# Reordering the seven down products of a fp32 decoder trunk, with the next layer's value weights spread over two of them

## The chip, the cores and the metric

One NeuronCore of a Trainium2 chip runs the whole program. The metric is the device time of one execution in microseconds, lower is better; the median of the runs is compared.

## The reference

The program computes two decoder layers for 512 tokens of width 1024 in float32. Each layer normalizes its input, projects it, runs differential attention and forgetting attention, projects back, normalizes and adds; then comes the FFN, and only its last line and the norm around it matter here:

```python
h = rms_norm(x, ffn_pre_g[l])
y = (jax.nn.silu(h @ w_gate[l]) * (h @ w_up[l])) @ w_down[l]
x = x + rms_norm(y, ffn_post_g[l])
```

With `D_FF` = 2816, the down projection is a 512 x 2816 by 2816 x 1024 product. The next layer begins with `h = rms_norm(x, attn_pre_g[l + 1])` and the projection of the value heads, `va`.

## The kernel before

Every float32 operand is split in a high part (`fp32r`) and a low part, the rest. ScalarE (ACT) makes the high part with a cast, VectorE (DVE) the low part with a subtraction (`load_w`, lines 258 and 259, for weights; `split`, lines 263 and 264, for the rest), and TensorE (PE) runs three matmuls for each product: high by high, high by low, low by high.

The down product is done as seven products of half size (Strassen's scheme in Winograd's form): the 2816 rows of the weight and the hidden activations are cut in two halves of 11 blocks, the tokens in two halves of 256 and the output columns in two of 512. Sums of activations are made while gate and up run (`swiglu`, from line 1236); some stay in SBUF as operands `op0q` to `op3q`, the others go to DRAM (`s_d`) and come back with `reload` (line 1326) into the operand buffers that have been read. Sums of weight blocks lie in DRAM (`t_d`), made by `weight_sums`.

A product (line 1320) runs over six chunks of weights (`chunk_w`, line 1297): five of two blocks (128 x 1024) and one of one block. A chunk's 12 matmuls (6 for the last) are 6 for the first 128 tokens of the half, m = 0, then 6 for m = 1; 66 in a product. The code's call `product(banks, g, x)` names the two PSUM banks, the operand group g and the weight side x. In the trace the matmuls are `da`, `db` or `dc` by the banks `A_`, `B_` or `C_`. In the order of a program below, a chunk is named by layer, side and number: `wl_d073` is the low part of chunk 3 of side 7 in layer 0. Even chunks are loaded into two buffers `wr`, odd ones into two buffers `xr`; high and low parts have three buffers each, so that the cast of a chunk waits for the PE to finish the chunk three before it. For the first four products `xr` shares the two buffers of the gains (tag `gain`); for the later ones `xr` takes the operand buffers `op32` and `op33`, which the fourth product reads.

The seven products stand in the code in this order (group, side): (0, 4) in `A_`, (1, 6) in `C_`, (2, 1) in `A_`, (3, 0) in `B_`, (0, 2) in `A_`, (1, 7) in `B_`, (2, 3) in `A_`. Below they are the first to the seventh product. Between them DVE adds banks into half tiles `u`, `u3`, `p5`, `y2`, which end as the four blocks of the result: the first 256 tokens (t = 0 and 1) have their second column half when the sixth product is done, and the last 256 tokens (t = 2 and 3) get theirs with the sixth and seventh.

`post_norm` (line 304) then sums the squares on ACT (`square_sum`, line 277), lets GpSimd (POOL) make the root in two steps (lines 271 and 272, `v` and `r`), and adds the scaled result to the residual `xs` on DVE (line 316); in the last layer each half is stored from there. `pre_norm` (line 279) does the same for the next layer's input (`h_a`, line 286), and `pre_T` transposes it on PE.

The last three chunks of the seventh product (`TAIL = 3`) run first for m = 0 and then for m = 1. After them come the 96 matmuls of the next layer's `va`, four token tiles t by four pieces c of the weight. Those weights are loaded (`wvr`) and split (`wvh`, `wvl`) into operand buffers that are free by then, named by `VA_TAGS`: for each of the four pieces c the buffer of the raw data, of the high and of the low part. In the next layer `vd_split` reads the banks of `va` into `vd_h` (ACT, line 386) and `vd_l` (DVE, line 387), which gives the four banks free for the projections (`pj_kd` is the first).

All instructions of an engine run in the order in which they were built; the tile framework's scheduler chooses that order from the code's order and its own costs. All loads are issued by SyncE (SP), in its own order too.

Of the kernel before, what the change touches and what calls it, by code (L numbers as in the profile page):

```python
# [11 lines left out]
F32 = mybir.dt.float32  # L12
# [23 lines left out]
TB = S // 16  # L36
VA_C, VA_T = 4, 1
TAIL = 3
VA_TAGS = (("34", "02", "03"), ("34", "04", "10"), ("30", "11", "12"), ("34", "13", "14"))
KSPLIT = 4  # L40
EPS = 1e-6
BIG = 1e30
# [132 lines left out]
def hymba_block(ctx, tc, x_d, pos_d, apre_d, win_d, fb_d, lq1_d, lk1_d, lq2_d, lk2_d, dsg_d, wout_d, apost_d,  # L175
# [171 lines left out]
    for l in range(DEPTH):  # L347
# [849 lines left out]
        with ExitStack() as fctx:  # L1197
# [155 lines left out]
                V.tensor_add(u[m], A_[m], u[m])  # L1353
            reload(1, 1)
            product(B_, 3, 0)
            p5, y = (hp.tile([P, 2, S], F32, name=f"{x}{l}", tag=f"op3{q}") for q, x in enumerate(("p5", "y0")))
            g_fpost = gain(fpost_d, l, f"g_fpost{l}")
            if l + 1 < DEPTH:
                g_apre = gain(apre_d, l + 1, f"g_apre{l + 1}")
            for m in range(2):  # L1360
                A.copy(p5[:, m], B_[m])
            reload(2, 2)
            for t in range(2):
                ys[t] = y[:, t]
                V.tensor_mul(ys[t], c11[t], g_fpost[:, CH[0]])
            product(A_, 0, 2)
            u3, y2 = (hp.tile([P, 2, S], F32, name=f"{x}{l}", tag=f"op0{q}") for q, x in enumerate(("u3", "y2")))
            for m in range(2):
                V.tensor_add(u3[:, m], A_[m], u[m])
                V.tensor_add(u[m], p5[:, m], u[m])  # L1370
            product(B_, 1, 7)
            last = l + 1 == DEPTH
            for m in range(2):
                V.tensor_add(u[m], B_[m], u[m])
            for t in range(2):
                post_norm(t, u[t], s2s[t], g_fpost, name, y=ys[t], store=last)
                if not last:
                    hs[t] = pre_norm(t, g_apre, f"a{l + 1}")
            for m in range(2):
                ys[2 + m] = y2[:, m]  # L1380
                V.tensor_add(ys[2 + m], u3[:, m], p5[:, m])
                s2s[2 + m] = first_half(2 + m, ys[2 + m], name, z=1)
                V.tensor_mul(ys[2 + m], ys[2 + m], g_fpost[:, CH[1]])
            product(A_, 2, 3, range(QN - TAIL))
            ws = [chunk_w(3, q) for q in range(QN - TAIL, QN)]
            if not last:
                for c in range(4):
                    raw, hi, lo = (hp.tile([P, 2, S], dt, name=f"wv{x}{l}{c}", tag=f"op{tag}") for x, dt, tag in zip(
                        "rhl", (F32, F32R, F32R), VA_TAGS[c]))
                    src = win_d[l + 1][2 * c * P:(2 * c + 2) * P, VA:VA + S].rearrange("(k p) n -> p k n", p=P)  # L1390
                    nc.sync.dma_start(raw, src)
                    split(hi, lo, raw)
                    for k in range(2):
                        wva[2 * c + k] = hi[:, k], lo[:, k]
            pinned[0] = True
            a = f"a{l + 1}"
            for m in range(2):
                t = 2 + m
                for w, q in zip(ws, range(QN - TAIL, QN)):
                    product_mm(A_[m], 2, q, w, m)  # L1400
                    if m and not last and q == QN - TAIL:
                        pre_T(0, hs[0], a)
                c21 = half_tile(f"c21{l}{m}")
                V.tensor_add(c21, A_[m], u3[:, m])
                post_norm(t, c21, s2s[t], g_fpost, name, z=0, y=ys[t], store=last)
                if not last:
                    hs[t] = pre_norm(t, g_apre, a)
            if not last:
                va(0, 0, 1)
                pre_T(1, hs[1], a)  # L1410
# [29 lines left out]
```

## Time and profile before

| what | us |
|---|---|
| three runs | 1244.06, 1246.26, 1253.99 |
| median | 1246.26 |
| the profiled execution | 1249.71 |
| its span, first to last instruction | 1247.9 |

The profiled execution is 3.45 us above the median, and 1.8 us of it lie around the span. PE is busy 96% of the span. Busy time of PE is modelled from the matmuls' issue, so a stretch in which PE counts as busy can still be longer than its matmuls need; the start of the first matmul of one product to the start of the first of the next is the measure used below.

### The profile page before, as it was taken

What the parts mean: (1) busy time and instruction counts of PE and PEld (TensorE: products, weight loads), DVE (VectorE), ACT (ScalarE), POOL (GpSimd) and SP (SyncE); (2) the same over time, 40 slices, a digit from 0 to 9 for tenths busy, and PEclk for the clock granted to TensorE, in tenths of its full rate; (3) what the DMA queues carried; (4) which work ended last, traced back from release to release, by engine and by line L of the source; (5) the groups of instructions that cost most, each with busy time, mean ns of one, the idle gap of its engine ahead of it and who ended that gap; (6) DMA issues with size and microseconds to landing.
All of it is one profiled execution on the core that took longest, in us unless ns stands there. A gap on an engine that the chain in (4) does not pass through costs nothing.

```text
span 1247.9 us, 16724 instructions
## 1 busy us (share of the span) xinstructions
PE 1201.7 (96%) x5817; PEld 989.3 (79%) x5817; DVE 817.3 (65%) x1574; ACT 599.2 (48%) x1162; POOL 210.4 (17%) x250
## 2 busy tenths in 40 slices
PE   8999999999999999999799999999999999999996
PEld 5787877788888888887687878777988888887875
DVE  7697858665554545576848977695755455555855
ACT  5476757553333233365544767674533233324643
POOL 1302457320000000000223124572200000000001
PEclk9999999999999999999999999999999999999999
DMA  7333443416575766798504333434167676677863
GB/s 231 91 85 93 112 115 105 136 37 196 188 238 182 227 203 211 251 313 264 171 2 119 90 89 93 121 110 125 62 192 242 196 214 212 208 233 247 294 203 125
DMA packets 211268, 206.75 MB, mean 166 GB/s; under 512 B 11680, under 2 KB 155680, under 8 KB 211184
## 3 DMA queue, kind: packets, MB, share of 16 engines
q1 hardware_dynamic: 211040, 205.16, 53.2%
q8 instruction: 46, 0.75, 0.3%
q10 hardware_dynamic: 144, 0.52, 0.1%
q14 instruction: 38, 0.31, 0.1%
HBM read 163.34 MB, written 33.91 MB: 158 GB/s over the span
## 4 chain that ended last, share of the span: by engine, by line
PE 44%; issue 32%; DVE 13%; ACT 4%; DMA 4%; POOL 2%; SPq 0%; POOLq 0%; DVEq 0%; ACTq 0%
PE pj_g L205 10%; PE pj_u L205 10%; PE o L205 4%; PE va L205 3%; PE pj_kf L205 2%; PE pj_kd L205 2%; PE da L205 2%; PE pj_qf L205 2%; DMA rs<-s_d 2%; PE vb L205 1%; DVE t2kd L739 1%; PE db L205 1%; PE ptf L210 1%; DVE ed L958 1%; PE of L205 1%
## 5 line engine op out<-in xcount | busy, mean ns | idle before, releaser
L205 PE MATMUL pj_g<-hT_h,wh_g 128*128 128x512 f32 (+1 forms) x384 | 142.9, 372 | 0.0
L205 PE MATMUL pj_g<-hT_l,wh_g 128*128 128x512 f32 (+1 forms) x384 | 142.6, 371 | 0.0
L205 PE MATMUL pj_g<-hT_h,wl_g 128*128 128x512 f32 (+1 forms) x384 | 142.6, 371 | 0.0
L205 PE MATMUL pj_u<-hT_h,wh_u 128*128 128x512 f32 (+1 forms) x368 | 140.1, 381 | 0.0
L205 PE MATMUL pj_u<-hT_l,wh_u 128*128 128x512 f32 (+1 forms) x368 | 139.8, 380 | 0.0
L205 PE MATMUL pj_u<-hT_h,wl_u 128*128 128x512 f32 (+1 forms) x368 | 139.8, 380 | 0.0
L271 POOL TENSOR_SCALAR v_fp<-s_fp 128x1 f32<-128x1 f32 x8 | 5.2, 651 | 685.4 <-ACT junk L277 354.7
L259 DVE TENSOR_TENSOR wl_u<-wr_u,wh_u 128x1024 fp32r<-128x1024 f32 x44 | 53.9, 1225 | 98.5 <-ACT wh_u L258 98.5
L258 ACT CAST wh_g<-wr_g 128x1024 fp32r<-128x1024 f32 x44 | 46.4, 1054 | 145.9 <-PE pj_u L205 86.9
L205 PE MATMUL da<-wh_d,op 128*128 128x512 f32 x352 | 111.3, 392 | 2.1 <-ACT wh_d L258 2.1
L258 ACT CAST wh_u<-wr_u 128x1024 fp32r<-128x1024 f32 x44 | 46.3, 1053 | 135.4 <-PE pj_g L205 128.3
L1239 DVE TENSOR_TENSOR sg<-pj_u,sg 128x512 f32<-128x512 f32 x44 | 30.4, 690 | 80.8 <-PE pj_u L205 80.8
L205 PEld LDWEIGHTS pj_g<-hT_h,wh_g 128*128 128x128 f32 x384 | 72.4, 188 | 12.7
L205 PEld LDWEIGHTS pj_g<-hT_h,wl_g 128*128 128x128 f32 x384 | 72.2, 188 | 12.5
L205 PEld LDWEIGHTS pj_g<-hT_l,wh_g 128*128 128x128 f32 x384 | 72.3, 188 | 12.3
L205 PE MATMUL da<-wl_d,op 128*128 128x512 f32 x176 | 69.7, 396 | 10.9 <-DVE wl_d L259 10.9
L205 PEld LDWEIGHTS pj_u<-hT_h,wl_u 128*128 128x128 f32 x368 | 69.2, 188 | 13.2
L205 PEld LDWEIGHTS pj_u<-hT_h,wh_u 128*128 128x128 f32 x368 | 69.2, 188 | 13.1
L205 PEld LDWEIGHTS pj_u<-hT_l,wh_u 128*128 128x128 f32 x368 | 69.2, 188 | 12.9
L205 PEld LDWEIGHTS da<-wh_d,op 128*128 128x128 f32 x352 | 66.4, 189 | 16.4 <-ACT wh_d L258 2.9
L258 ACT CAST wh_d<-wr_d 128x1024 fp32r<-128x1024 f32 x42 | 44.2, 1052 | 42.4 <-PE da L205 15.4
L259 DVE TENSOR_TENSOR wl_d<-wr_d,wh_d 128x1024 fp32r<-128x1024 f32 x42 | 51.3, 1222 | 19.2 <-ACT wh_d L258 18.6
(301 smaller groups left out, 3019.1 us busy)
## 6 DMA issues: line engine op xcount, KB each, us to landing
wr_g<-in_w_gate_dram SPq DMA_DIRECT2D x44, 512.0 KB, 4.4
wr_u<-in_w_up_dram SPq DMA_DIRECT2D x44, 512.0 KB, 4.6
b<-in_w_down_dram SPq DMA_DIRECT2D x88, 256.0 KB, 3.6
t_d<-b SPq DMA_DIRECT2D x88, 256.0 KB, 4.0
wr_d<-t_d SPq DMA_DIRECT2D x24, 512.0 KB, 4.9
wr_d<-in_w_down_dram SPq DMA_DIRECT2D x18, 512.0 KB, 5.0
wr_o<-in_w_out_dram SPq DMA_DIRECT2D x16, 512.0 KB, 4.4
xr<-t_d SPq DMA_DIRECT2D x16, 512.0 KB, 5.1
```

The costliest lines, as they stand in the source:

```text
L205: ins = PE.matmul(out, a, b, start=start, stop=stop)
L210: ins = PE.transpose(out, a, idn)
L258: A.copy(hi, raw)
L259: (eng or V).tensor_sub(lo, raw, hi.bitcast(F32))
L271: G.tensor_scalar(v, s2[:, 0:1], scalar1=s2[:, 1:2], scalar2=EPS, op0=ALU.add, op1=ALU.add)
L739: return V.tensor_mul(b["t2"], b["t2"], sinT)
L958: return V.scalar_tensor_tensor(e0, e0, b["r"][:, 0:1], e1, op0=ALU.mult, op1=ALU.add)
L1239: V.tensor_mul(sg, pu, sg)
```

## The change

The last three products become (1, 7) in `C_`, (0, 2) in `B_`, (2, 3) in `A_`. The first 256 tokens are whole after the fifth product. The copy `p5` and the tiles `u3` and `y2` go; `w5` holds the sum of the fourth product and `u`, and `c12` the finished column half of the first tokens. The norm of t = 0 and the value pieces 0 and 1 stand in the code before the sixth product's sums are read, the norm of t = 1 and the pieces 2 and 3 behind the seventh product's chunks. The pieces take other operand buffers.

```diff
-VA_TAGS = (("34", "02", "03"), ("34", "04", "10"), ("30", "11", "12"), ("34", "13", "14"))
+VA_TAGS = (("34", "10", "11"), ("14", "12", "13"), ("34", "00", "01"), ("04", "02", "03"))
...
             product(B_, 3, 0)
-            p5, y = (hp.tile([P, 2, S], F32, name=f"{x}{l}", tag=f"op3{q}") for q, x in enumerate(("p5", "y0")))
+            w5, y = (hp.tile([P, 2, S], F32, name=f"{x}{l}", tag=f"op3{q}") for q, x in enumerate(("w5", "y0")))
+            for m in range(2):
+                V.tensor_add(w5[:, m], B_[m], u[m])
+            reload(2, 2)
+            product(C_, 1, 7)
             g_fpost = gain(fpost_d, l, f"g_fpost{l}")
...
-                A.copy(p5[:, m], B_[m])
-            reload(2, 2)
-            for t in range(2):
-                ys[t] = y[:, t]
-                V.tensor_mul(ys[t], c11[t], g_fpost[:, CH[0]])
-            product(A_, 0, 2)
-            u3, y2 = (hp.tile([P, 2, S], F32, name=f"{x}{l}", tag=f"op0{q}") for q, x in enumerate(("u3", "y2")))
-            for m in range(2):
-                V.tensor_add(u3[:, m], A_[m], u[m])
-                V.tensor_add(u[m], p5[:, m], u[m])
-            product(B_, 1, 7)
...
+                ys[m] = y[:, m]
+                V.tensor_mul(ys[m], c11[m], g_fpost[:, CH[0]])
+                V.tensor_add(c12[m], C_[m], w5[:, m])
+            product(B_, 0, 2)
+            a = f"a{l + 1}"
+
+            def end(t, x, z):
+                post_norm(t, x, s2s[t], g_fpost, name, z=z, y=ys[t], store=last)
                 if not last:
-                    hs[t] = pre_norm(t, g_apre, f"a{l + 1}")
...
+            end(0, c12[0], 1)
+            values_w(0, 1)
+            for m in range(2):
+                ys[2 + m] = w5[:, m]
+                V.tensor_add(ys[2 + m], B_[m], w5[:, m])
+                V.tensor_add(u[m], B_[m], u[m])
+            product(A_, 2, 3, range(QN - TAIL))
+            ws = [chunk_w(3, q) for q in range(QN - TAIL, QN)]
+            end(1, c12[1], 1)
+            values_w(2, 3)
+            for m in range(2):
+                s2s[2 + m] = first_half(2 + m, ys[2 + m], name, z=1)
+                V.tensor_mul(ys[2 + m], ys[2 + m], g_fpost[:, CH[1]])
...
-                V.tensor_add(c21, A_[m], u3[:, m])
+                V.tensor_add(c21, A_[m], u[m])
```

`values_w(*cs)` holds the loop over the pieces that stood there before, word for word. Where the instructions now stand is shown at three places, before first and after second.

SP in layer 0, from the first chunk of the fifth product on: `wr`, `xr` are weight chunks, `rs` the reloaded operands, `g_` the gains, `wvr` the value weights.

```order
L257 DMA wr_d020_5485<-t_d0_3047 128x2x512
L1331 DMA rs024_5473<-s_d0_3048 128x2x256
L236 DMA g_fpost0_5447<-in_ffn_post_g_dram 128x1024
L1331 DMA rs025_5478<-s_d0_3048 128x256
L257 DMA wr_d022_5521<-t_d0_3047 128x2x512
L236 DMA g_apre1_5449<-in_attn_pre_g_dram 128x1024
L257 DMA xr021_5503<-t_d0_3047 128x2x512
L257 DMA xr023_5539<-t_d0_3047 128x2x512
```

```order
L257 DMA wr_d070_5479<-in_w_down_dram 128x2x512
L1331 DMA rs024_5469<-s_d0_3048 128x2x256
L1331 DMA rs025_5474<-s_d0_3048 128x256
L257 DMA wr_d072_5515<-in_w_down_dram 128x2x512
L257 DMA xr071_5497<-in_w_down_dram 128x2x512
L257 DMA xr073_5533<-in_w_down_dram 128x2x512
L257 DMA wr_d074_5551<-in_w_down_dram 128x2x512
L1383 DMA wvr00_5716<-in_w_in_dram 128x2x512
```

The two gains went from ahead of the second chunk to behind the sixth; the first value piece follows the fifth chunk.

DVE in layer 0 during the sixth product (`wl_d07` before, `wl_d02` after): `wvl` are value pieces, `y1_fp`, `xs` and `h_a` the steps of a token tile's norms.

```order
L259 TENSOR_TENSOR wl_d073_5649<-xr073_5647,wh_d073_5648 128x1024
L1381 TENSOR_TENSOR y20_5588<-u30_5587,p50_5445 128x512 x2
L264 TENSOR_TENSOR wvl01_5833<-wvr01_5831,wvh01_5832 128x1024
L259 TENSOR_TENSOR wl_d074_5667<-wr_d074_5665,wh_d074_5666 128x1024
L259 TENSOR_TENSOR wl_d075_5685<-xr075_5683,wh_d075_5684 128x512
```

```order
L259 TENSOR_TENSOR wl_d023_5647<-xr023_5645,wh_d023_5646 128x1024
L316 SCALAR_TENSOR_TENSOR xs_78<-y1_fp00_5695,r_fp00_5697,xs_78 128x512
L264 TENSOR_TENSOR wvl01_5724<-wvr01_5722,wvh01_5723 128x1024
L264 TENSOR_TENSOR wvl02_5829<-wvr02_5827,wvh02_5828 128x1024
L259 TENSOR_TENSOR wl_d024_5665<-wr_d024_5663,wh_d024_5664 128x1024
L259 TENSOR_TENSOR wl_d025_5683<-xr025_5681,wh_d025_5682 128x512
L286 SCALAR_TENSOR_TENSOR h_a100_5703<-xs_78,r_a10_5710,g_apre1_5583 128x512
L286 SCALAR_TENSOR_TENSOR h_a101_5704<-xs_78,r_a10_5710,g_apre1_5583 128x512
L313 TENSOR_TENSOR y1_fp01_5806<-c1201_5586,g_fpost0_5581 128x512
```

The norm of the first token tile and half of that of the second have come into this product, and so has one more value piece.

DVE in layer 0 from the first chunk of the seventh product (`wl_d030`) on.

```order
L259 TENSOR_TENSOR wl_d030_5755<-wr_d030_5753,wh_d030_5754 128x1024
L264 TENSOR_TENSOR wvl03_5845<-wvr03_5843,wvh03_5844 128x1024
L1374 TENSOR_TENSOR u00_5063<-db00_4959,u00_5063 128x512
L1374 TENSOR_TENSOR u01_5064<-db01_4960,u01_5064 128x512
L313 TENSOR_TENSOR y1_fp00_5699<-u00_5063,g_fpost0_5447 128x512
L259 TENSOR_TENSOR wl_d031_5773<-xr031_5771,wh_d031_5772 128x1024
L316 SCALAR_TENSOR_TENSOR xs_78<-y00_5446,r_fp00_5701,xs_78 128x512
L316 SCALAR_TENSOR_TENSOR xs_78<-y1_fp00_5699,r_fp00_5701,xs_78 128x512
L259 TENSOR_TENSOR wl_d032_5791<-wr_d032_5789,wh_d032_5790 128x1024
```

```order
L259 TENSOR_TENSOR wl_d030_5734<-wr_d030_5732,wh_d030_5733 128x1024
L316 SCALAR_TENSOR_TENSOR xs_78<-y1_fp01_5806,r_fp01_5808,xs_78 128x512
L1392 TENSOR_TENSOR w50_5445<-db00_4959,w50_5445 128x512
L1393 TENSOR_TENSOR u00_5063<-db00_4959,u00_5063 128x512
L1392 TENSOR_TENSOR w50_5445<-db01_4960,w50_5445 128x512
L1393 TENSOR_TENSOR u01_5064<-db01_4960,u01_5064 128x512
L259 TENSOR_TENSOR wl_d031_5752<-xr031_5750,wh_d031_5751 128x1024
L259 TENSOR_TENSOR wl_d032_5770<-wr_d032_5768,wh_d032_5769 128x1024
L286 SCALAR_TENSOR_TENSOR h_a110_5814<-xs_78,r_a11_5821,g_apre1_5583 128x512
```

Ahead of the second chunk's low part there now stand four adds that read the sixth product's banks; the steps of the norms behind it are fewer.

## Rows read from the trace of the kernel before

**Rows 1.** Stretches: us; busy PE, PEld, DVE, ACT, POOL (instructions); PEclk, DMA share, GB/s.
```profile
572.53:590.25 17.72, 15.56 (x67) 12.31 (x66) 8.34 (x8) 8.27 (x10) 0.00 (x0) 1.00 0.81 263
590.25:605.22 14.97, 14.97 (x68) 12.39 (x66) 11.17 (x14) 7.32 (x8) 0.00 (x0) 1.00 0.84 275
605.22:630.46 25.24, 18.94 (x75) 14.17 (x74) 20.32 (x27) 13.90 (x30) 7.44 (x10) 0.93 0.26 78
625.00:630.00 5.00, 5.00 (x20) 4.24 (x19) 3.74 (x6) 2.77 (x7) 0.86 (x2) 0.66 0.00 0
1189.72:1206.67 16.95, 15.50 (x67) 12.31 (x66) 7.21 (x7) 7.70 (x9) 0.00 (x0) 1.00 0.57 185
1221.63:1239.98 18.35, 15.27 (x67) 12.12 (x65) 13.20 (x18) 7.08 (x14) 3.85 (x6) 1.00 0.28 98
```

**Rows 2.** Waits of PE, 560 to 660 us, then 1150 to 1250: total, times, longest.
```profile
PE da L205 <- DVE wl_d L259: 7.1, 6, 2.4
PE da L205 <- ACT wh_d L258: 1.4, 1, 1.4
...
PE da L205 <- DVE wl_d L259: 3.8, 2, 3.1
```

**Rows 3.** Timeline of PE: start, us, line, tiles, count, idle before and releaser.
```profile
623.97 0.50 PE L205 MATMUL da<-wl_d,op 128*128 128x512 f32 x1 [2.42 <-DVE wl_d L259]
...
625.71 0.63 PE L205 MATMUL da<-wl_d,op 128*128 128x512 f32 x1
...
633.18 1.03 PE L210 MATMUL hp_a<-con,h_a 128*128 128x128 f32 x8
```

**Rows 4.** Timeline of SP, of ACT, and the chain of waits: one load each.
```profile
567.70 0.37 SPq L257 DMA_DIRECT2D wr_d<-t_d  x1
...
569.29 0.94 SPq L257 DMA_DIRECT2D xr<-t_d  x2
...
575.71 1.04 ACT L258 CAST wh_d<-xr 128x1024 fp32r<-128x1024 f32 x1 [3.07 <-DMA xr<-t_d]
...
1184.63 7.46 DMA xr<-t_d
```

**Rows 5.** The page's DMA issues: tiles, count, KB each, median us to landing.
```profile
wr_d<-in_w_down_dram SPq DMA_DIRECT2D x18, 512.0 KB, 5.0
```

**Rows 6.** Timeline of DVE in layer 0, at the end of the fifth product and in the seventh.
```profile
589.77 0.69 DVE L1369 TENSOR_TENSOR u<-da,u 128x512 f32<-128x512 f32 x1 [0.98 <-PE da L205]
...
607.14 1.28 DVE L1374 TENSOR_TENSOR u<-db,u 128x512 f32<-128x512 f32 x2
608.34 0.68 DVE L313 TENSOR_TENSOR y_fp<-u,g_fpost 128x512 f32<-128x512 f32 x1
...
610.92 0.75 DVE L316 SCALAR_TENSOR_TENSOR xs<-y,r_fp,xs 128x512 f32<-128x512 f32 x1 [0.76 <-POOL r_fp L272]
611.59 0.74 DVE L316 SCALAR_TENSOR_TENSOR xs<-y_fp,r_fp,xs 128x512 f32<-128x512 f32 x1
612.25 1.22 DVE L259 TENSOR_TENSOR wl_d<-wr_d,wh_d 128x1024 fp32r<-128x1024 f32 x1
613.39 1.22 DVE L259 TENSOR_TENSOR wl_d<-xr,wh_d 128x1024 fp32r<-128x1024 f32 x1
615.37 1.42 DVE L286 SCALAR_TENSOR_TENSOR h_a<-xs,r_a,g_apre 128x512 f32<-128x512 f32 x2 [0.76 <-POOL r_a L272]
```

**Rows 7.** Timeline of POOL: the root's first step, twice.
```profile
608.68 1.56 POOL L271 TENSOR_SCALAR v_fp<-s_fp 128x1 f32<-128x1 f32 x1 [331.61 <-ACT junk L277]
...
626.35 0.30 POOL L271 TENSOR_SCALAR v_fp<-s_fp 128x1 f32<-128x1 f32 x1 [5.69 <-ACT junk L277]
```

**Rows 8.** The tile wvr: landing of its four loads; ACT's longest wait for one.
```profile
DMA to landing us min/median/max: 5.6/5.8/7.3
...
602.64 1.05 ACT L263 CAST wvh<-wvr 128x1024 fp32r<-128x1024 f32 x1 [3.40 <-DMA wvr<-in_w_in_dram]
```

**Rows 9.** Timeline at the end of va: vd_l, then the first projection.
```profile
654.82 1.89 DVE L387 TENSOR_TENSOR vdl<-va,vdh 128x512 fp32r<-128x512 f32 x3 [5.20 <-PE va L205]
...
656.13 0.39 PE L205 MATMUL pj_kd<-hT_h,wh_kd 128*128 128x512 f32 x1
```

More of the change, by code (lines that the diff above doesn't have):

```diff
@@ L1355, in hymba_block @@
             product(B_, 3, 0)
-            p5, y = (hp.tile([P, 2, S], F32, name=f"{x}{l}", tag=f"op3{q}") for q, x in enumerate(("p5", "y0")))
+            w5, y = (hp.tile([P, 2, S], F32, name=f"{x}{l}", tag=f"op3{q}") for q, x in enumerate(("w5", "y0")))
[3 more added lines that the diff above has]
+            product(C_, 1, 7)
             g_fpost = gain(fpost_d, l, f"g_fpost{l}")
-            if l + 1 < DEPTH:
+            last = l + 1 == DEPTH
@@ L1359, in hymba_block @@
+            if not last:
                 g_apre = gain(apre_d, l + 1, f"g_apre{l + 1}")
+            c12 = [half_tile(f"c12{l}{m}") for m in range(2)]
             for m in range(2):
-                A.copy(p5[:, m], B_[m])
-            reload(2, 2)
-            for t in range(2):
-                ys[t] = y[:, t]
-                V.tensor_mul(ys[t], c11[t], g_fpost[:, CH[0]])
-            product(A_, 0, 2)
-            u3, y2 = (hp.tile([P, 2, S], F32, name=f"{x}{l}", tag=f"op0{q}") for q, x in enumerate(("u3", "y2")))
@@ L1368, in hymba_block @@
-            for m in range(2):
-                V.tensor_add(u3[:, m], A_[m], u[m])
-                V.tensor_add(u[m], p5[:, m], u[m])
-            product(B_, 1, 7)
[L1372 to L1376, printed above, removed]
-                if not last:
-                    hs[t] = pre_norm(t, g_apre, f"a{l + 1}")
[L1379 to L1387, printed above, removed]
+                ys[m] = y[:, m]
[5 more added lines that the diff above has]
+                post_norm(t, x, s2s[t], g_fpost, name, z=z, y=ys[t], store=last)
+                if not last:
+                    hs[t] = pre_norm(t, g_apre, a)
@@ L1388, in hymba_block, with values_w @@
+            def values_w(*cs):
+                for c in () if last else cs:
                     raw, hi, lo = (hp.tile([P, 2, S], dt, name=f"wv{x}{l}{c}", tag=f"op{tag}") for x, dt, tag in zip(
@@ L1394, in hymba_block @@
                         wva[2 * c + k] = hi[:, k], lo[:, k]
+            end(0, c12[0], 1)
[11 more added lines that the diff above has]
+                V.tensor_mul(ys[2 + m], ys[2 + m], g_fpost[:, CH[1]])
             pinned[0] = True
-            a = f"a{l + 1}"
             for m in range(2):
@@ L1403, in hymba_block @@
                 c21 = half_tile(f"c21{l}{m}")
-                V.tensor_add(c21, A_[m], u3[:, m])
-                post_norm(t, c21, s2s[t], g_fpost, name, z=0, y=ys[t], store=last)
-                if not last:
-                    hs[t] = pre_norm(t, g_apre, a)
+                V.tensor_add(c21, A_[m], u[m])
+                end(t, c21, 0)
             if not last:
```

## Prediction

> **What bounds the kernel now.** I read the stretches by stage first. The bare length of a product is the one that ran without a wait: the sixth of layer 0 took 14.97 us for 66 matmuls, 0.227 us each [rows 1]. By that measure the fifth product of layer 0 lost 17.72 - 14.97 = 2.75 us. The seventh took 25.24 us; it holds eight transposes besides, about 1.0 us [rows 3], so it lost 9.3 us. In layer 1 the fifth product lost 16.95 - 14.97 = 1.98 us and the seventh, without transposes, 18.35 - 14.97 = 3.38 us. Together PE lost 17.4 us in the five places that the change touches, 1.4% of the span; elsewhere it does not touch the time.
>
> The waits say what was missing there: the low part of a weight chunk, from DVE, 7.1 us in six waits in layer 0 and 3.8 us in two in layer 1, and once the high part [rows 2]. In the seventh product this is no lack of weights but of DVE: it was busy 20.32 of 25.24 us, while it was busy 11.17 of 14.97 us in the sixth and 8.34 of 17.72 us in the fifth [rows 1]. Both token tiles' norms came due at once when the sixth product was done, and the splits of the weights stood behind them in DVE's order. In the fifth product it is a load: ACT waited 3.07 us for the chunk `xr` that SP had issued at 569.29 us [rows 4]. The seventh product's loss is more than its waits because the granted clock fell as well: 0.93 over the product and 0.66 in the five microseconds behind the last long wait, and a matmul took 0.63 us there [rows 1, 3].
>
> **The fifth product.** What is added and removed in work is small: the two copies `p5` leave ACT, DVE makes eight adds per layer as before, the loads are the same in number and size. What counts is the order on SP. In layer 0 the second chunk was issued at 569.29 us, behind both gains; the chunk ahead of it went out at 567.70 us [rows 4]. Now it follows that one directly, so it is issued 1.2 us sooner, at 568.07 us, and 1 MB of gains is not in front of it. PE starts the product at 572.53 us and needs this chunk's low part 13 matmuls later, at 575.5 us; cast and subtraction take 1.05 + 1.22 us [rows 4, 6], so it must have landed by 573.2 us. With the median landing of 5.0 us [rows 5] it lands at 573.1 us; with the 6.4 us it took before (569.29 to 575.71) it would stall PE 1.3 us. I take 0.5 us, bounds 0 and 1.4. In layer 1 the issue stays where it was, at 1184.63 us, and the load took 7.46 us [rows 4] to 1192.1 us; it had to be there at 1189.72 + 2.95 - 2.27 = 1190.4 us. One gain, 512 KB, leaves the front of it, which at the 263 to 275 GB/s of these stretches [rows 1] is 1.9 us. That lands it at 1190.2 us: I take 0.3 us of stall, bounds 0 and 2.0.
>
> **The sixth product.** In layer 0 DVE gets here what it did later. From the first add that reads the fifth product to the low part of the seventh product's second chunk it has, by the starts of one and the next [rows 6]: seven splits of 1024 columns at 1.14 us (five of weights, two of values) 7.98, one short split 0.6, eight adds and gain products at 0.60 us 4.8, four steps of `xs` at 0.66 us 2.64, two of `h_a` 1.4, and the last split 1.22; together 18.6 us. It begins 0.48 us ahead of the product's end before, as at 589.77 us against 590.25 us [rows 6, 1], and the last split is wanted 14.97 + 13 x 0.227 = 17.92 us after the product's start. So the list fills the time: 18.1 against 17.9 us. Within the product each chunk's split comes in time by this list (the fifth chunk's is done at 9 to 10 us and wanted at 11.1 us), so I put its loss at 0.
>
> **The seventh product.** In layer 0 the end of that list is the stall: 0.2 us, and what DVE waits for POOL's root in between. Before, DVE waited 0.76 us for such a root twice [rows 6]. In the new order other work lies in the gap; I count one such wait, so 1.0 us, bounds 0 and 3.5 (all four roots late). Behind it the chunks have room: the norm of the second tile is half done, one value piece remains, and its split stands between the two last chunks. The clock then has no reason to fall, since the longest wait is under the 1.4 us after which it stayed at 1.00 in the fifth product [rows 1, 2]. In layer 1 no values are loaded and the norms of both tiles fit in the sixth product; only the four adds, 2.4 us from 0.48 us ahead of the product's start, and the split of 1.22 us stand against 2.95 us: 0.2 us. The eight stores of the last layer now stand between loads on SP, but each of the first four waits for an `xs` step that stands on DVE ahead of the split which frees the buffer of the load behind it, so no load waits longer for it. The tail behind the last matmul is unchanged.
>
> **A wait that is new.** The pieces of the value weights change places. In the two built programs the next layer's `vd_l` lies on the buffers `op02` and `op12`, `vd_h` on `op00` and `op10`. Before, `op12` held the low part of piece 2, so `vd_l` could start when the last tile's matmuls on piece 2 were done, at 654.82 us, 1.3 us before `pj_kd` at 656.13 us [rows 9]. Now `op02` holds piece 3, the last one, so `vd_l` starts at the end of `va`, 1.36 us (six matmuls) later, and `pj_kd` takes the bank that the first `vd_l` reads. Its subtraction of 0.69 us and the hand-overs are uncovered: 0.75 us lost. That is read from both built programs, and I give it bounds 0.6 and 1.0.
>
> **The sum.** Layer 0: 2.75 + 9.3 = 12.05 us lost before, 0.5 + 1.0 + 0.75 = 2.25 us after, gain 9.8. Layer 1: 5.36 us before, 0.3 + 0.2 after, gain 4.9. Together 14.7 us: the profiled execution would go from 1249.71 to 1235.0 us. It stands 3.45 us above the median of the runs shown; against that median the forecast is 1246.26 - 14.7 = 1231.6 us.
>
> **A rule that speaks against it.** POOL's first step took 1.56 us at 608.68 us, while DVE subtracted one SBUF tile from another, and 0.30 us at 626.35 us, while DVE was idle [rows 7]. The Trainium skill, "SBUF — State Buffer", section "Who interferes with whom", says that a DVE instruction with two SBUF inputs and a GpSimd instruction that reads SBUF exclude each other for the whole instruction. The two rows agree with it; by it, all eight steps of the two norms in the sixth product would be slow there, which is the first rival below.
>
> **Rivals.** *Late roots.* DVE's list has no slack, so each wait for a root goes through to PE. If all four cost 0.8 us as the two seen, the stall is 3.4 instead of 1.0 us: 1234.0 us. For it: the two waits; against it: the scheduler put a split or a product between the square sum and the step in three of four places. *Values late, the stalls move.* ACT casts a value piece ahead of weight chunks in the fifth, sixth and seventh products, and waited 3.40 us for one such load; they take up to 7.3 us to land [rows 8]. In an order where DVE is full from the fifth product's end on, two such waits of 3.4 us put back 5 to 7 us: about 1237.5 us. Against it: each piece is issued as soon as its buffer is free, and only piece 1 (free with the fifth chunk of the fifth product) and piece 3 (with the fifth of the sixth) come close to the casts behind them. *The clock.* If stalls of two microseconds follow one another at the start of the seventh product, as before at its end, the granted clock drops there and not behind it, and with it the 66 matmuls left and the 96 of `va`: at 0.63 instead of 0.39 us each [rows 3], 0.20 us more from start to start, that is 162 x 0.20 = 32 us, or 1264 us, slower than now. It decides only if the low clock lasts; before, it was back at 1.00 within a few microseconds while the matmuls ran on, and nothing in the new order makes two long waits in a row. The Trainium skill, "TensorE: Matmul & The Clock Gate", Part 1, says the same of the direction: an idle array is given half the clock, a busy one gets it back.
>
> **How the numbers follow.** The forecast's mechanism has a chance of 0.62, with its own range of 1228.5 to 1235 us (all bounds at their good ends give a gain of 16.6 us, 1229.6 us). Late roots 0.17, late values 0.17, the clock 0.04. A measurement of this kernel tells about 1% from no change, 12.5 us, that is below 1233.8 us. Nearly all of the first case and some of the second lie under it: 0.62 faster, 0.34 within, 0.04 slower. The range for 8 in 10 is 1227.5 to 1240 us.
>
> **What would show it.** In the changed profile: the fifth product 15.0 to 15.5 us from first to last start in both layers, and no gain among the loads that are under way when its second chunk is issued; the sixth 15.0 us with DVE at 14 us or more in layer 0; the seventh 17 us in layer 0 and 15.2 in layer 1, with one wait for the second chunk's low part; PEclk 1.00 there; a wait of `pj_kd` for DVE's `vd_l` of 0.75 us. I am wrong if the sixth product shows waits of several microseconds, if ACT waits for `wvr` with weight casts behind it, or if the seventh still takes over 20 us.

## The result, and the profile after

The changed kernel takes 1233.8 us (median of four runs, 1232.99 to 1236.11) where the kernel before takes 1247.62 us in the runs beside it (1244.06 to 1253.99): a ratio of 0.989 with a 95% interval of 0.9863 to 0.9917, 13.8 us faster (the interval allows 10 to 17). The forecast was 1231.6 us and a gain of 14.7 us; the times alone can't tell 13.8 from 14.7, so the stages have to. The profiled execution took 1233.1 us, its span is 1231.3 us.

The stretches of the changed kernel come first, as in [rows 1]: length, busy time of PE, PEld, DVE, ACT and POOL with the instructions in brackets, then PEclk, DMA share and GB/s. They are the fifth, sixth and seventh product and `va` of layer 0, then the three products of layer 1.

```profile
569.45:584.41 14.96, 14.96 (x67) 12.39 (x66) 10.18 (x12) 6.96 (x8) 0.00 (x0) 1.00 0.98 331
584.41:599.37 14.96, 14.96 (x67) 12.39 (x66) 13.35 (x17) 9.54 (x16) 6.73 (x6) 1.00 0.64 230
599.37:617.18 17.81, 16.48 (x76) 13.06 (x74) 15.58 (x21) 10.37 (x20) 1.73 (x4) 1.00 0.45 133
617.18:644.64 27.46, 25.68 (x122) 20.12 (x120) 11.17 (x18) 11.41 (x22) 7.36 (x8) 1.00 0.07 20
1178.02:1193.27 15.25, 15.25 (x68) 12.31 (x66) 9.05 (x11) 6.84 (x7) 0.00 (x0) 1.00 0.73 245
1193.27:1208.23 14.96, 14.96 (x68) 12.39 (x66) 11.60 (x15) 7.24 (x10) 5.18 (x4) 1.00 0.76 245
1208.23:1223.34 15.11, 15.11 (x67) 12.13 (x65) 10.53 (x14) 5.85 (x10) 0.86 (x2) 1.00 0.20 68
```

The fifth product of layer 0 has gone from 17.72 to the bare 14.96 us, the seventh from 25.24 to 17.81, those of layer 1 from 16.95 to 15.25 and from 18.35 to 15.11 [rows 1]. DVE's busy time tells how: in layer 0 it fell from 20.32 to 15.58 us in the seventh product and rose from 11.17 to 13.35 us in the sixth. The granted clock is 1.00 throughout. The stretch of `va` became longer, 27.46 us where it was 25.67 (630.46 to 656.13 us in the trace of before).

The waits of PE from 560 to 660 us show what is left (total, times, longest), in place of the 7.1 us in six waits of [rows 2]; from 1150 to 1250 us, where there were 3.8 us, none is left at all.

```profile
PE da L205 <- DVE wl_d L259: 1.3, 2, 1.0
PE pj_kd L205 <- DVE vdl L387: 0.9, 1, 0.9
PE va L205 <- DVE hT_l L264: 0.7, 1, 0.7
```

In the timeline of PE these are four stalls; the second column is the duration, the bracket the idle time before.

```profile
600.13 0.50 PE L205 MATMUL da<-wl_d,op 128*128 128x512 f32 x1 [0.37 <-DVE wl_d L259]
...
604.32 0.50 PE L205 MATMUL da<-wl_d,op 128*128 128x512 f32 x1 [0.95 <-DVE wl_d L259]
...
625.06 0.50 PE L205 MATMUL va<-wvh,hT_l 128*128 128x512 f32 x1 [0.69 <-DVE hT_l L264]
...
644.64 0.50 PE L205 MATMUL pj_kd<-hT_h,wh_kd 128*128 128x512 f32 x1 [0.85 <-DVE vdl L387]
```

The first two are the low parts of the seventh product's first two chunks. DVE's timeline around them shows what stands ahead of the second one (603.06 us): an `xs` step and the four adds that read the sixth product.

```profile
598.87 1.21 DVE L259 TENSOR_TENSOR wl_d<-wr_d,wh_d 128x1024 fp32r<-128x1024 f32 x1
600.00 0.73 DVE L316 SCALAR_TENSOR_TENSOR xs<-y_fp,r_fp,xs 128x512 f32<-128x512 f32 x1
600.67 0.67 DVE L1392 TENSOR_TENSOR w<-db,w 128x512 f32<-128x512 f32 x1
...
602.46 0.67 DVE L1393 TENSOR_TENSOR u<-db,u 128x512 f32<-128x512 f32 x1
603.06 1.21 DVE L259 TENSOR_TENSOR wl_d<-xr,wh_d 128x1024 fp32r<-128x1024 f32 x1
```

The roots of the norms, [rows 7], now fall into the sixth product, beside DVE's subtractions. POOL's first step took 1.79 and 2.12 us there, and 0.30 us at 601.65 us, where DVE does the adds that read one operand from a bank of PSUM. DVE waited for two of the roots:

```profile
586.38 1.79 POOL L271 TENSOR_SCALAR v_fp<-s_fp 128x1 f32<-128x1 f32 x1 [312.39 <-DVE c L1369]
...
593.46 2.12 POOL L271 TENSOR_SCALAR v_a<-ss_a 128x1 f32<-128x1 f32 x1 [4.64 <-ACT junk L277]
...
601.65 0.30 POOL L271 TENSOR_SCALAR v_a<-ss_a 128x1 f32<-128x1 f32 x1 [3.55 <-ACT junk L277]
```

```profile
588.86 0.75 DVE L316 SCALAR_TENSOR_TENSOR xs<-y,r_fp,xs 128x512 f32<-128x512 f32 x1 [0.76 <-POOL r_fp L272]
...
596.26 1.42 DVE L286 SCALAR_TENSOR_TENSOR h_a<-xs,r_a,g_apre 128x512 f32<-128x512 f32 x2 [0.85 <-POOL r_a L272]
```

Last, SP's timeline at the fifth product of layer 0, as in [rows 4]. The second chunk (`xr`) goes out right behind the one ahead of it, and the gains follow 7.5 us later:

```profile
563.29 0.37 SPq L257 DMA_DIRECT2D wr_d<-in_w_down_dram  x1
563.71 2.22 SPq L257 DMA_DIRECT2D xr<-in_w_down_dram  x2
...
571.21 0.43 SPq L236 DMA_DIRECT2D g_fpost<-in_ffn_post_g_dram  x1
```

The spans of the two profiled executions differ by 1247.9 - 1231.3 = 16.6 us, the medians by 13.8. The difference can be read off the starts: from the fifth product's start to `pj_kd` the changed kernel takes 644.64 - 569.45 = 75.19 us, before 656.13 - 572.53 = 83.60 us, so 8.4 us less. In layer 1 it is 1223.34 - 1178.02 = 45.32 against 1239.98 - 1189.72 = 50.26 us, 4.9 us less. That is 13.35 us, which fits the medians. Of the other 3.3 us, 3.08 lie ahead of the fifth product's first start in layer 0 (572.53 against 569.45 us), where PE runs the same instructions in the same order. About 2 us of that are the clock: from 210 to 240 us PE ran 131 matmuls at a granted clock of 0.94 before and 140 at 1.00 after, nine of 0.227 us. How far this start varies from one execution to the next, the experiments show.

### The profile page after: what moved, and what is told of

It reads as the page before. It is cut to its first block, busy times and chain, and to the rows that moved or that the text cites. A ratio compares the mean times of both kernels' runs of the same rounds, so it can differ in the third digit from the quotient of the medians.

```text
span 1231.3 us, 16721 instructions
## 1 busy us (share of the span) xinstructions
PE 1195.3 (97%) x5817; PEld 987.0 (80%) x5817; DVE 816.5 (66%) x1574; ACT 597.1 (48%) x1158; POOL 214.1 (17%) x250
## 4 chain that ended last, share of the span: by engine, by line
PE 76%; DVE 11%; issue 7%; ACT 3%; POOL 2%; DMA 1%; POOLq 0%; DVEq 0%; SPq 0%; ACTq 0%
PE pj_g L205 20%; PE pj_u L205 19%; PE o L205 5%; PE da L205 5%; PE dc L205 5%; PE va L205 3%; PE pj_kd L205 3%; PE pj_kf L205 2%; PE db L205 2%; PE pj_qf L205 2%; PE vb L205 1%; DVE t2kd L739 1%; PE of L205 1%; PE pj_qd L205 1%; PE ptf L210 1%
## 5 line engine op out<-in xcount | busy, mean ns | idle before, releaser
L205 PE MATMUL da<-wh_d,op 128*128 128x512 f32 x264 | 82.6, 390 | 0.0
L258 ACT CAST wh_d<-xr 128x1024 fp32r<-128x1024 f32 (+1 forms) x42 | 38.1, 908 | 43.7 <-PE da L205 13.2
L205 PEld LDWEIGHTS da<-wh_d,op 128*128 128x128 f32 x264 | 49.6, 188 | 10.2
```

The lines of the kernel that those rows point to most:

```text
L205: ins = PE.matmul(out, a, b, start=start, stop=stop)
L258: A.copy(hi, raw)
```

## The experiments

The stages are given by the starts of their first matmuls. The kernel before ran beside each group: its median is 1248.03 us beside e1 to e4, 1246.38 beside e5 to e8 and 1246.25 beside e9 to e11 (the numbers in the labels).

**Undoing the order of the products.** The old order, with gains, values and sums as changed.

```diff
-VA_TAGS = (("34", "10", "11"), ("14", "12", "13"), ("34", "00", "01"), ("04", "02", "03"))
+VA_TAGS = (("34", "00", "01"), ("04", "02", "03"), ("34", "10", "11"), ("14", "12", "13"))
-            product(C_, 1, 7)
+            product(B_, 0, 2)
...
-                V.tensor_add(c12[m], C_[m], w5[:, m])
-            product(B_, 0, 2)
+            product(C_, 1, 7)
+            for m in range(2):
+                V.tensor_add(c12[m], C_[m], w5[:, m])
```

> The changed kernel with the fifth and the sixth product in the old order (and the value pieces on the buffers that then come free first), gains, values and sums else as changed. Theory (DVE's list at the seventh product): both token tiles' norms come due with the sixth product's end again; DVE's work in the seventh product of layer 0 goes from 15.6 to 19 us and the product from 17.8 to 21 us (19 to 25), in layer 1 from 15.1 to 17 to 18.4 us; together 5 us slower than the changed kernel (3 to 10), fifth and sixth at 15.0. Rival (the gains' place and the values made the difference): the seventh stays at 18.5 us or less in layer 0 and 15.5 us or less in layer 1.

Measured: 1244.69 us, ratio 0.9982 (0.996 to 1.0004), about 11 us above the changed kernel's 1233.8, where 3 to 10 were forecast. The seventh product took 23.12 us in layer 0 and 17.59 in layer 1, with one wait of 4.15 and one of 2.33 us. But the fifth took 16.90 and 16.74 us, which the theory had not in it: here it writes the banks that the fourth product has just left, and PE waited for the add that reads them (0.20 us) and then for a low part that DVE did behind the adds (0.76 us). So I exchanged the banks too:

```diff
-            product(B_, 0, 2)
+            product(C_, 0, 2)
...
-            product(C_, 1, 7)
+            product(B_, 1, 7)
...
```

The adds read the exchanged banks.

> As e4_swap (old order of the fifth and sixth product, everything else of the changed kernel), with the banks exchanged as well, so that the fifth product does not write the banks that the fourth one just left. Theory (the order matters by the norms that come due together; the fifth product's loss in e4_swap came from the shared banks): fifth and sixth product at 15.0 to 15.3 us in both layers, the seventh again 22 to 23 us in layer 0 and 17.4 us in layer 1; 7 to 9 us slower than the changed kernel. Rival (the fifth product of the old order is slow by itself, its weights coming later): 16.7 to 16.9 us for it as in e4_swap, 11 us slower.

Measured: 1241.15 us, ratio 0.9963 (0.9944 to 0.9983); the changed kernel beside it took 1231.52 us, so the old order costs 9.6 us, somewhat over the forecast of 7 to 9. Its profile is of the slowest of its ten executions (1245.03 us). The stretches (fifth, seventh and `va` of layer 0, fifth and seventh of layer 1):

```profile
571.02:585.98 14.96, 14.96 (x67) 12.39 (x66) 9.82 (x12) 7.91 (x8) 0.00 (x0) 1.00 1.00 341
600.94:622.67 21.73, 17.57 (x75) 14.21 (x74) 18.46 (x26) 11.29 (x24) 4.30 (x8) 0.92 0.35 108
622.67:651.50 28.83, 26.10 (x121) 20.04 (x119) 12.85 (x21) 12.56 (x25) 8.51 (x10) 1.00 0.07 19
1186.63:1202.74 16.11, 15.35 (x68) 12.31 (x66) 8.64 (x11) 6.73 (x7) 0.00 (x0) 1.00 0.73 250
1217.70:1235.29 17.59, 15.25 (x67) 12.12 (x65) 15.49 (x22) 7.09 (x14) 3.86 (x6) 1.00 0.29 101
```

Layer 0's fifth product is bare again, so its loss in the first form was the banks. The seventh products and `va` carry (21.73 - 17.81) + (28.83 - 27.46) + (17.59 - 15.11) = 7.8 us; in layer 0's seventh a part of it is the clock, 0.92 with the long wait. Another 0.9 us is in layer 1's fifth product, where a load landed late (16.11 us), as it does in profiles of other kernels below. DVE's timeline in the seventh product of layer 0 shows the mechanism in one piece: from the sum `c` on, norm steps, adds and two waits for roots stand ahead of the third chunk's low part, and PE waited 4.16 us for it.

```profile
604.34 0.75 DVE L316 SCALAR_TENSOR_TENSOR xs<-y,r_fp,xs 128x512 f32<-128x512 f32 x1 [0.85 <-POOL r_fp L272]
...
608.55 1.42 DVE L286 SCALAR_TENSOR_TENSOR h_a<-xs,r_a,g_apre 128x512 f32<-128x512 f32 x2 [0.41 <-POOL r_a L272]
609.89 1.21 DVE L259 TENSOR_TENSOR wl_d<-wr_d,wh_d 128x1024 fp32r<-128x1024 f32 x1
```

**The gains alone, in the kernel before.**

```diff
-            g_fpost = gain(fpost_d, l, f"g_fpost{l}")
-            if l + 1 < DEPTH:
-                g_apre = gain(apre_d, l + 1, f"g_apre{l + 1}")
...
             product(A_, 0, 2)
+            g_fpost = gain(fpost_d, l, f"g_fpost{l}")
+            if l + 1 < DEPTH:
+                g_apre = gain(apre_d, l + 1, f"g_apre{l + 1}")
...
```

The two multiplications that read the gain (`tensor_mul`) move with it.

> The kernel before, with the loads of the gains (and the products y that read them) behind the fifth product's chunks, nothing else moved in the source. Theory (the load): the fifth product goes from 17.7 to 15.0-15.5 us in layer 0 and from 17.0 to 15.0-15.3 us in layer 1, the sixth stays at 15.0, the seventh at 25 and 18.4 us, as the norms still come due together: 4.0 to 4.7 us faster in all, 0.9965 of before. Rival (the copies): p5 stands on ACT ahead of the second chunk's cast and that is what delays it; then the fifth product keeps 1 us or more of its loss in both layers.

Measured: 1243.68 us, 4.35 us less than before, ratio 0.9974 (0.995 to 0.9998). Fifth and seventh product of layer 0, then of layer 1:

```profile
570.48:585.81 15.33, 15.33 (x68) 12.24 (x66) 9.37 (x10) 8.66 (x10) 0.00 (x0) 1.00 0.84 304
600.77:624.04 23.27, 17.33 (x76) 12.83 (x75) 18.87 (x26) 12.79 (x28) 7.44 (x10) 1.00 0.31 88
1183.76:1198.82 15.06, 15.06 (x68) 12.31 (x67) 8.33 (x9) 7.70 (x9) 0.00 (x0) 1.00 0.73 240
1213.78:1234.99 21.21, 18.14 (x67) 14.27 (x65) 13.19 (x18) 7.08 (x14) 3.85 (x6) 0.84 0.24 84
```

The fifth products lost 2.4 and 1.9 us less: the load was the cause. The copies `p5` did not move in the source; on ACT one of them stood ahead of the second chunk's cast before and stands behind it here, but behind that copy ACT still sat idle for 3.07 us until the load landed [rows 4], so the copy held nothing up. The seventh products show something else. In layer 0 it took 2.0 us less than before with the same longest waits (2.00 and 2.41 us here, 2.01 and 2.42 there), at a granted clock of 1.00 instead of 0.93; in layer 1 it took 2.9 us more than before with the same one wait, at 0.84. The matmuls behind that wait, here and then in the kernel before:

```profile
1222.90 0.80 PE L205 MATMUL da<-wl_d,op 128*128 128x512 f32 x1 [3.07 <-DVE wl_d L259]
1223.49 1.06 PE L205 MATMUL da<-wh_d,op 128*128 128x512 f32 x2
1224.35 0.63 PE L205 MATMUL da<-wl_d,op 128*128 128x512 f32 x1
```

```profile
1230.77 0.50 PE L205 MATMUL da<-wl_d,op 128*128 128x512 f32 x1 [3.08 <-DVE wl_d L259]
1231.10 0.63 PE L205 MATMUL da<-wh_d,op 128*128 128x512 f32 x2
1231.56 0.40 PE L205 MATMUL da<-wl_d,op 128*128 128x512 f32 x1
```

A stall of 3.1 us was followed by the lower clock in one execution and not in the other. These two executions paid for the clock in different layers; how often it falls where, two executions do not show.

**The gains, put back ahead in the changed kernel.**

```diff
+            g_fpost = gain(fpost_d, l, f"g_fpost{l}")
+            last = l + 1 == DEPTH
+            if not last:
+                g_apre = gain(apre_d, l + 1, f"g_apre{l + 1}")
             product(C_, 1, 7)
-            g_fpost = gain(fpost_d, l, f"g_fpost{l}")
...
```

> The changed kernel with the loads of the gains ahead of the fifth product's loads again. Theory (the load has a margin now): the second chunk was in DVE 0.7 to 1.2 us before it was wanted, one gain costs 1.9 us of transfer, so 0 to 1 us returns in layer 0 and 0 to 2 us in layer 1, 1.0 us in all. Rival (the place of the gains was the whole of the loss): 2.75 and 1.98 us return, 4.7 us in all; the fifth product is 17.7 and 17.0 us again.

Measured: 1233.81 us, ratio 0.9916 (0.9888 to 0.9944): by the time no change. By the stages 0.7 us came back in layer 0 (15.68 us): 0.2 at the second chunk and 0.5 at the fifth, whose low part stood on DVE behind a value piece that ACT had waited 2.25 us for. Layer 1's 15.88 us says nothing of the gains, since kernels of the new order that load them late took 14.96 to 15.90 us there. In this order SP issued `xr` between the two gains and not behind both. The gains' place was worth 4.3 us before, and in the new order about 0.7 us.

**The spread of the values.** Three pieces share one raw buffer, as before the change.

```diff
-VA_TAGS = (("34", "10", "11"), ("14", "12", "13"), ("34", "00", "01"), ("04", "02", "03"))
+VA_TAGS = (("34", "12", "13"), ("34", "14", "00"), ("31", "01", "02"), ("34", "03", "04"))
```

> The changed kernel with the value pieces on the buffers of the kernel before, mirrored to the new order of the products: three of the four share one raw buffer, so their loads follow one another. Theory (the number of splits counts, not their spread): DVE has the same four splits, two of them by the sixth product's end as before this edit; the seventh product of layer 0 takes 17.5 to 19.5 us, the wait of pj_kd for vdl goes since the last piece lies elsewhere, and the time is within 2 us of the changed kernel, 0.988 to 0.991 of before. Rival (the spread of the values was a main part of the gain): with serial loads the last pieces come late, DVE or va waits several microseconds for wvr, and 4 us or more return.

Measured: 1230.43 us, ratio 0.9868 (0.982 to 0.9916). Seventh product and `va` of layer 0:

```profile
598.34:616.12 17.78, 16.26 (x75) 13.06 (x74) 15.59 (x21) 10.00 (x19) 2.12 (x4) 1.00 0.46 131
616.12:642.63 26.51, 25.63 (x121) 20.30 (x120) 11.73 (x19) 10.92 (x21) 7.34 (x8) 1.00 0.05 13
```

The seventh is the same to 0.03 us, `va` is 0.95 us shorter without the wait of `pj_kd`. The spread of the values gave nothing of the gain; the rival falls.

**The address behind the new wait.**

```diff
-VA_TAGS = (("34", "10", "11"), ("14", "12", "13"), ("34", "00", "01"), ("04", "02", "03"))
+VA_TAGS = (("34", "10", "11"), ("14", "12", "13"), ("34", "00", "01"), ("04", "14", "03"))
```

> The changed kernel with the last value piece on the buffers op14 and op03 instead of op02 and op03; the order of instructions on every engine stays. Theory (an address): vd_l waits for the last piece because it lies on op02; then the wait of pj_kd for vdl, 0.85 us, goes, and va to the start of pj_kd takes 27.46 - 1.1 = 26.3 us, all other stages as in the changed kernel. Rival (the eviction): vd_l is late because ACT's copy of the bank and the subtraction follow the last matmul of va in any case; then pj_kd still waits 0.8 to 0.9 us.

Measured: 1233.62 us, ratio 0.99 (0.9864 to 0.9936). No wait of PE is left at `pj_kd`, and `va` to its start took 26.69 us, 0.8 less: the address it was. 0.2 us are left of the 1.0, between the last matmul of `va` (647.02) and the start.

```profile
646.70 1.89 DVE L387 TENSOR_TENSOR vdl<-va,vdh 128x512 fp32r<-128x512 f32 x3 [5.98 <-ACT vdh L386]
...
647.02 0.39 PE L205 MATMUL va<-wvh,hT_l 128*128 128x512 f32 x1
...
647.45 0.50 PE L205 MATMUL pj_kd<-hT_h,wh_kd 128*128 128x512 f32 x1
```

The same profile shows what a late root costs. Every engine runs the same instructions in the same order as in the changed kernel, but in this execution the root's first step that took 2.12 us there took 1.38 us, and DVE waited 0.45 us for that root and not 0.85:

```profile
597.52 1.38 POOL L271 TENSOR_SCALAR v_a<-ss_a 128x1 f32<-128x1 f32 x1 [4.78 <-ACT junk L277]
...
599.87 1.42 DVE L286 SCALAR_TENSOR_TENSOR h_a<-xs,r_a,g_apre 128x512 f32<-128x512 f32 x2 [0.45 <-POOL r_a L272]
```

The seventh product took 17.46 us, 0.35 less, and its first chunk's wait is no longer among those listed. In the repeat of the changed kernel below DVE waited 0.85 us again and the product took 17.77 us. So a wait of DVE for a root in the sixth product reaches PE almost whole.

**The four adds, behind the second chunk.**

```diff
-            for m in range(2):
-                ys[2 + m] = w5[:, m]
-                V.tensor_add(ys[2 + m], B_[m], w5[:, m])
-                V.tensor_add(u[m], B_[m], u[m])
             product(A_, 2, 3, range(QN - TAIL))
             ws = [chunk_w(3, q) for q in range(QN - TAIL, QN)]
+            for m in range(2):
...
```

> The changed kernel with the four adds that read the sixth product written behind the seventh product's loads, so that DVE does the second chunk's low part after the first of them. Theory (DVE's list is the stall): the wait of 0.95 us for the second chunk's low part goes, and 1.2 us with it; the seventh product of layer 0 takes 16.0 to 16.7 us instead of 17.8, layer 1 stays at 14.9. Rival (the work only changes places): a wait of the same size comes with the third or fourth chunk, whose low part now stands behind the adds, and the seventh stays at 17.4 us or more.

Measured: 1232.28 us, ratio 0.9877 (0.9832 to 0.9923). The seventh product took 16.55 us, 1.26 us less; the wait of 0.95 us is gone and none took its place. In the kernel before only two adds read the sixth product's banks [rows 6], since the first finished half of the last 256 tokens (`y2`, from `u3` and `p5`) was whole with the fifth product and not with the sixth; the new sums brought two more to this place. Here one add instead of four stands on DVE between the `xs` step and the second chunk's low part:

```profile
604.44 0.68 DVE L1394 TENSOR_TENSOR w<-db,w 128x512 f32<-128x512 f32 x1
605.04 1.21 DVE L259 TENSOR_TENSOR wl_d<-xr,wh_d 128x1024 fp32r<-128x1024 f32 x1
```

**The root's first step on DVE.**

```diff
-        G.tensor_scalar(v, s2[:, 0:1], scalar1=s2[:, 1:2], scalar2=EPS, op0=ALU.add, op1=ALU.add)
+        (V if name[:2] == "fp" or name[0] == "a" else G).tensor_scalar(
+            v, s2[:, 0:1], scalar1=s2[:, 1:2], scalar2=EPS, op0=ALU.add, op1=ALU.add)
```

> The changed kernel with the first step of the roots of both norms at the layer's end (128 sums, one column) on DVE instead of POOL, where it took 1.79 and 2.12 us beside DVE's subtractions. Theory (late roots cost part of the stall): the step takes 0.1 to 0.2 us on DVE, its waits for r_fp and r_a in the sixth product (0.76 and 0.85 us) go, the low parts of the seventh product's first two chunks come 1.5 us sooner, and both stalls (0.37 and 0.95 us idle, 1.9 us by starts) shrink to under 0.5 us. Rival (the wait moves into DVE's queue): DVE now waits for ACT's sum of squares at the step itself, as long as it had waited for the root, and the stalls stay.

Measured: 1237.35 us, ratio 0.9934 (0.9907 to 0.9961). The condition also takes in the norm behind attention, and there PE waited 4.7 us in four waits for `h_f`, so the time says nothing of the layer's end and only its stages count. The step took 0.21 us on DVE, and both waits for roots in the sixth product went, as did the first stall. But DVE waited for ACT in their place (0.25 and 0.67 us for casts, 0.16 us for a square sum) and 0.66 us for a root in the seventh product, 1.74 us where it had waited 1.61. The second stall grew from 0.95 to 1.69 us, and the seventh took 17.86 us.

```profile
603.86 0.21 DVE L271 TENSOR_SCALAR v_fp<-s_fp 128x1 f32<-128x1 f32 x1
604.73 0.75 DVE L317 SCALAR_TENSOR_TENSOR xs<-y,r_fp,xs 128x512 f32<-128x512 f32 x1 [0.66 <-POOL r_fp L273]
...
607.79 1.22 DVE L259 TENSOR_TENSOR wl_d<-xr,wh_d 128x1024 fp32r<-128x1024 f32 x1
```

The rival held: the waits changed places, and the four adds stand right ahead of the late low part here too. That the first stall went is no sign of the roots. The scheduler also put an `xs` step (0.66 us), which stood ahead of the first chunk's low part at 598.21 us in the changed kernel, behind it; that is most of the 0.82 us by which this low part starts sooner, 1.32 us ahead of the product and not 0.50.

**Transposes one place sooner.**

```diff
-                    if m and not last and q == QN - TAIL:
-                        pre_T(0, hs[0], a)
+                    if not last and q == (QN - TAIL if m else QN - 1):
+                        pre_T(m, hs[m], a)
...
-                va(0, 0, 1)
-                pre_T(1, hs[1], a)
-                va(0, 2, 3)
+                va(0, 0, 1, 2, 3)
```

> The changed kernel with the transposes of the first token tile at the end of the third tile's last products and those of the second tile where the first tile's stood (one place sooner each). Theory (the new wait of va for hT_l is DVE busy with the norm of the fourth tile): hT_l of the second tile is done before va wants it, the wait of 0.65 to 0.69 us goes, and the stage of va, now without these eight transposes, takes 25.3 us instead of 27.5 while the seventh product takes 1.0 us more for them; 1.0 us faster in all. Rival (DVE has no room): the splits of hT_l now stand ahead of the third and fourth tile's norm steps, and PE waits for their h_a before the transposes of these tiles instead; nothing gained.

Measured: 1235.45 us, ratio 0.9899 (0.9844 to 0.9953). The wait for `hT_l` is gone and `va` takes 25.38 us, the seventh 19.07: together 44.45 us instead of 45.27. PE did not wait for the third tile's `h_a`. The theory held; the gain is 0.8 us in these two stages, of which 0.3 went again in the sixth product (15.25 us), and it is too small for the times.

**All three together, beside the changed kernel itself.** The edits of the pieces, the adds and the transposes at once, and the changed kernel unchanged.

> The changed kernel with three edits together, which were tried alone: the last value piece on op14 and op03, the four adds behind the seventh product's loads, the transposes of the first two tiles one place sooner. If the three stalls are separate, their gains by stages add up: 1.26 us in the seventh product (e6_adds_late), 0.8 to 1.1 us at pj_kd (e1_pieces), 0.5 to 0.8 us for the transposes (e7_transposes_sooner), 2.6 to 3.2 us in all: 1231 us where the changed kernel takes 1233.8. Rival (they share DVE's idle time): the transposes' splits push the third tile's norm, PE waits for it in va, and the gain is 1 to 2 us.

> The changed kernel itself once more, on the chip and in the rounds of the two kernels beside it. The stages of both layers' ends repeat to 0.1 us (fifth and sixth product 14.96, seventh 17.5 to 17.8 in layer 0 and 14.9 in layer 1, va 27.5), and the time is 1233 to 1235 us; what differs from the first profile lies in other stages, where the granted clock is below 1.00. Rival (the stages themselves vary from run to run by 1 us or more): then stage differences under 1 us between the experiments tell nothing.

Measured: 1231.85 us, ratio 0.9891 (0.9873 to 0.9909), and 1231.52 us, ratio 0.99 (0.9877 to 0.9923), for the changed kernel. By the stages the three gains do add up: from the fifth product's start to `pj_kd` 643.67 - 571.21 = 72.46 us against 644.73 - 569.53 = 75.20, 2.7 us less. The changed kernel's stages repeat to 0.1 us in layer 0; only layer 1's fifth product does not (15.25 us in its first profile, 14.96 here, 15.90 with the three edits). By the time nothing is seen, and in the two profiled executions the reason stands in a stretch that no edit touches, in attention. The kernel with the three edits, then the changed kernel:

```profile
210.00:240.00 30.00, 26.71 (x127) 20.91 (x127) 24.95 (x54) 18.10 (x41) 16.54 (x16) 0.94 0.47 155
```

```profile
210.00:240.00 30.00, 28.40 (x146) 22.45 (x147) 26.10 (x58) 20.06 (x44) 18.20 (x17) 1.00 0.51 158
```

In the same 30 us the one got through 127 matmuls at a granted clock of 0.94, the other through 146 at 1.00. The fifth product of layer 0 starts at 568.4 to 573.9 us in the profiles of these kernels (the one with other roots in attention left out), at 569.5 and 573.4 us in two (the repeat and the edit of one address) whose order ahead of it is the same. A difference of 2.7 us cannot be seen in a handful of times with such a spread, so no version is shown to beat the changed kernel; the 9.6 us of the order can.

## Why the prediction was right

By its own steps, forecast against measurement:

- *The fifth product*, 0.5 and 0.3 us of loss: 0 in layer 0, 0.3 in layer 1. The cause, a chunk behind the gains, is shown by moving them alone. Of "so it is issued 1.2 us sooner": set against the product's start, `xr` went out 569.29 - 572.53 = -3.2 us before, 566.03 - 570.48 = -4.45 us with the gains alone moved, and 563.71 - 569.45 = -5.7 us after. So the gains' share is the 1.2 us. The rest comes from the chunk ahead of `xr`, which SP issues when DVE has read its buffer, and that varies: in the edit of one address, with the same order on every engine, `xr` went out 568.80 - 573.38 = -4.6 us. The fifth product took 14.96 us there too, so going out 1.2 us sooner is enough, and the 0.5 us of loss was too much.
- *The sixth product*, no loss: 14.96 us. DVE was busy for 13.35 us there, under the 14 I had named.
- *The seventh product of layer 0*, 1.0 us of loss: 17.81 - 14.97 - 1.0 = 1.8 us, in two stalls. The list was right: from its first add (583.93 us) to the end of the second chunk's low part (604.27 us) DVE took 20.3 us, 18.7 of them work, where 18.6 were counted. The term that was too small is "I count one such wait": two roots were late (0.76 and 0.85 us), the rival of the late roots half come true, and the edit of one address shows that such a wait reaches PE. I also took the list as it stood; the four adds in it (2.4 us) need not stand ahead of the second chunk.
- *The new wait* of `pj_kd`, 0.75 us: 0.85 us idle, and 0.8 us of the stage went with the address. Right in cause, and in size within its bounds.
- *Not foreseen*: the wait of `va` for `hT_l`, 0.69 us. PE reaches the second tile's transposes sooner, DVE is then busy with the fourth tile's norm; the transposes put sooner took it away.
- *Layer 1*, 4.9 us: 4.9.
- *The sum*: layer 0 gave 8.4 us instead of 9.8 (0.5 us better in the fifth product, 0.8 worse in the seventh, 1.0 worse in `va`), both layers 13.35 instead of 14.7, the medians 13.8. The 17.4 us that the prediction puts in five places are the sum of four stages.
- *The lower clock* was counted as part of the loss before, 2.0 us of the 9.3 in layer 0. The gain-only run, with the same longest waits, paid nothing for it there but 2.9 us in layer 1. To count it once in the sum fits both executions; that it holds on average is not shown. The rival that it would take hold did not happen: 1.00 in all stretches.
- *Values late* did not happen: ACT waited once for a piece, 0.8 us, where it had waited 3.40 [rows 8]; the serial loads of the old buffers were no worse than the spread ones.

Of the change's three parts, the order of the products carries it: 9.6 us by undoing it. The change without its order (the old order with exchanged banks) is 1246.25 - 1241.15 = 5.1 us faster than the kernel before, about what the later gains give there by themselves (4.35 us). The value pieces' new places give nothing, and cost 0.8 to 0.95 us by one address. What a part is worth hangs on the others: in the new order the gains' place is worth only about 0.7 us.

The Trainium skill's rule that I weighed ("SBUF — State Buffer", section "Who interferes with whom") bears out in both directions: POOL's first step took 1.79 and 2.12 us beside DVE's subtractions of two SBUF tiles, and 0.30 us beside its adds with one operand in PSUM.

## What to carry to other kernels

When two engines share a deadline, look for what comes due at the same moment and ask which input could be whole earlier: reordering two independent products here spread DVE's work over a stretch in which it had room, without removing any of it. Ahead of a late operand, list what stands before it in that engine's order and which of it is needed later, before blaming the last releaser: moving four adds was worth 1.26 us, moving the root's first step to DVE nothing. And price an edit of a few microseconds by its stages, since another stretch of the same program can vary by as much from one execution to the next. A stage varies too, if less: the seventh product took 17.46 to 17.81 us in three profiles of one order, so a smaller difference wants a repeat.

## What the runs showed of the hardware that was not expected

A stall of PE costs more than its idle time. At 600.13 us the idle time is 0.37 us, but from the matmul ahead (599.37 us) to the next but one behind (600.47) it is 1.10 us instead of 2 x 0.227: 0.65 us lost. The first matmul after idle time took 0.50 instead of 0.39 us, and the next started 0.34 us later instead of 0.227. The other part of the loss is how idle time is counted: the matmul ahead counts as busy for 0.39 us, while the next one normally starts 0.227 us behind its start.

The same wait of 3.1 us was followed by the full clock in one execution (0.40 us a matmul) and by the lower in another (0.63 us, and 2.9 us in all). And in the stretch from 210 to 240 us, which no edit touches, the mean granted clock was 0.94 or 1.00, 1.00 being the level of 2.4 GHz and 0.94 a mean with some time at 1.2 GHz in it, which with what lies ahead moved the start of the layer's end by up to 4 us between kernels of one order. What decides which of them happens, no run here shows.
